# Eight weight pieces of each sub-layer split in buffers of their own, and the products with 1/s spaced out

## The chip, the cores and the metric

The kernel runs on one core of one Trainium2 chip. The metric is the device time of one execution in microseconds. The kernel before takes 1218.72 us, the median of three runs (1218.52 to 1219.39). The profile and its trace come from one further execution of the same kernel.

## The reference

The reference is one inference step of a two-layer encoder trunk for two groups of tokens that share the weights: 256 prompt frames with 16 meta tokens ahead of them, and 32 frames of a running stream. Together that is N = 304 columns of activations with 1024 features, all in 32-bit floats. Cut to what matters:

```python
for l in range(DEPTH):                                     # DEPTH = 2
    x = x + 0.5 * rmsnorm(swiglu(rmsnorm(x, pre1) @ w1_in) @ w1_out, post1)   # D_FF = 2816
    z = rmsnorm(x, pre_mix) @ w_in                         # q, k, v of attention; q, k, v, gate of retention
    x = x + rmsnorm(concat(attention(z), retention(z)) @ w_out, post_mix)
    x = x + 0.5 * rmsnorm(swiglu(rmsnorm(x, pre2) @ w2_in) @ w2_out, post2)
y = rmsnorm(x, final_norm)
```

Attention is windowed, with 8 heads over 2 key/value heads and a learned sink per head. Retention has 8 heads with a decay per head and a state that is given and returned. Key and value caches and states are outputs too.

## The kernel before, in words

Activations lie transposed: features on the 128 partitions, the 304 columns of tokens along the free dimension. Layer 1 drops the 16 meta columns after its mixer's projections and goes on with 288. Each sub-layer (ffn1, mixer, ffn2 of each layer) is a row of groups of matmuls. `group4` makes four blocks of 128 output features over all blocks of input features; `group2` makes two.

Every product is computed in three matmuls, `mm3` (L234, L235, L237): the weight is split into `hi`, its rounded part, and `lo`, the rest, and so is the activation; hi·hi, lo·hi and hi·lo are summed in PSUM. A **piece** is one 128x512 block of weights, 12 matmuls. There are 648 pieces, in the fixed order of the program, two to a **chunk** of 512 KB. `load_to` issues the chunks from SP (L167, L171) into four `raw` buffers: a new chunk's load waits until the split of the chunk four before it is done. `split_one` splits a piece: ACT copies `raw` into `hi` (L183), then DVE subtracts to make `lo` (L186). `hi` and `lo` have ten buffers each, used in turn.

The order of the work is written out by hand: each engine's queue holds its instructions in the order in which the program issues them. `tick(ns)` is called between pieces with a nominal duration. It adds to a clock of the planner, issues up to two splits (`advance`) as long as no more than eight pieces are split and not yet used (`AHEAD`), and issues what is due in `later`, a list of things to do from a given value of that clock. The clock exists only while the program is built; on the chip nothing waits for it. `st["cap"]` keeps the splits back while a norm is under way.

Between sub-layers stands the norm. `Post` is its first half. While the last group of a sub-layer runs its last blocks, `done0` and `done1` take the squares on ACT (L488, L501; tiles `sq`, two buffers) and add them into `acc`, on POOL for the first four blocks (L491) and on DVE for the others (L503). `finish` sums `acc` over the partitions with matmuls by ones (L509, L510) and takes the root, s (L514). The matmuls of the next sub-layer start from x·s: `first` and `step` scale x by s (POOL, L523) and add the sub-layer's output, and `pre_norm` makes the split activations (`act_hi` L401, `act_lo` L404) and the next sum of squares. Because x is carried scaled by s, `unscale` (L545) multiplies it back with 1/s later: one reciprocal on DVE (L547) and eight products on POOL (L549). In the mixer it is due 3000 on the planner's clock after `gate_out`, so in the first of the two `w_out` groups; in an ffn, 3000 after the start of the down projections; in the last ffn, at the third gate/up group.

At the end of an ffn `hold` issues 12 matmuls (L271) that keep TensorE at work. At the end of the mixer the retention states are computed there instead (`states`, L787), and `state_out` sends them on during the next sub-layer, with four transfers between partitions on SP (L804).

In each ffn the hidden activations `hh`, `hl` and the temporaries stand in a pool `ffn`; in the mixer all tiles stand in a pool `mix`, which is closed by `after` when the next norm has been issued. Both pools follow one another in the same room.

Of the kernel before, what the change touches and what calls it, by code (L numbers as in the profile page):

```python
# [15 lines left out]
P = 128  # L16
# [50 lines left out]
UNSCALE = 3000  # L67
# [39 lines left out]
def tile_hybrid_step(ctx, tc, I, O):  # L107
# [35 lines left out]

    for l in range(DEPTH):
        ch_ffn_in(I["ffn1_w_in"][l])
        ch_cols(I["ffn1_w_out"][l], 512, KF)
        ch_cols(I["ffn1_w_out"][l], 0, KF)
        ch_qkv(I["w_in"][l])
        for c0 in (C_Q + 256, C_RK, C_RQ, C_RV, C_RK + 256, C_RQ + 256, C_RV + 256, C_G, C_G + 256):
            ch_pair(I["w_in"][l], c0)  # L150
        ch_cols(I["w_out"][l], 512, KD)
        ch_cols(I["w_out"][l], 0, KD)
        ch_ffn_in(I["ffn2_w_in"][l])
        ch_cols(I["ffn2_w_out"][l], 512, KF)
        ch_cols(I["ffn2_w_out"][l], 0, KF)

    raws, split = {}, {}
    st = {"dma": 0, "split": 0, "use": 0, "free": 0, "cap": 1 << 30, "ramp": 0}
# [318 lines left out]
    class Post:  # L477
# [67 lines left out]
        def unscale(self):  # L545
            rs = small("rs")
            DVE.reciprocal(out=rs[:, T0:], in_=self.s[:, T0:])  # L547
            for k in range(KD):
                POOL.tensor_tensor(out=x[:, k, T0:], in0=x[:, k, T0:], in1=rs[:, T0:], op=ALU.mult)  # L549


    def ffn(pre, post, nxt, prev, after=None):
# [5 lines left out]
        with tc.tile_pool(name="ffn", bufs=1, reuse_waits="tile") as fp:  # L558
# [3 lines left out]
            if last:  # L562
                fin.start(fp)
            state = {}
# [138 lines left out]
    def mixer(l, prev):  # L703
# [5 lines left out]
        mp = mix.enter_context(tc.tile_pool(name="mix", bufs=1, reuse_waits="tile"))  # L709
        def tl(name, shape, dt=F32, tag=None, bufs=1):  # L710
            return mp.tile(shape, dt, tag=tag or name, bufs=bufs, name=name)

# [30 lines left out]
        def rotate(bk, i, dst):  # L743
            t1 = tl("t1", [P, 2, N], bufs=2)
            t2 = tl("t2", [P, 2, N], bufs=1)
            t3 = tl("t3", [P, 2, N], bufs=1)
# [43 lines left out]
        def state_out(b):  # L790
            sa, sb = tl("t1", [P, 2, N], bufs=2), tl("t1", [P, 2, N], bufs=2)
            sc, stt = tl("t2", [P, 2, N]), tl("t3", [P, 2, N])
            sa, sb, sc, stt = (t.rearrange("p a n -> p (a n)")[:, 0:8 * HD].rearrange("p (w q d) -> p w q d", w=2, q=4)
                               for t in (sa, sb, sc, stt))
# [14 lines left out]
        def done_rv(i):  # L809
            def f(m, bk):  # L810
                zr = tl("zr", [P, N], bufs=2)
# [68 lines left out]
        def norm(p):  # L880
# [3 lines left out]
            sd = tl("gsd", [P, N], bufs=2)[:, t0:]  # L884
# [5 lines left out]
        def done_kv(m, bk):  # L890
            if m == 0:
                y = bk[0]
                zk = tl("zk", [P, N])
# [7 lines left out]
                def tr():  # L901
# [6 lines left out]
                    kt = tl("kt", [P, 2, P])  # L908
# [6 lines left out]
            else:  # L915
                zv = tl("zv", [P, N])
# [37 lines left out]
        def softmax(parts, rows):  # L954

            pt = tl("pt", [P, 2, 2, 208], bufs=2)
            sm = tl("sm", [P, 3, 2, 2], bufs=2)
# [22 lines left out]
        def attn_pair(g, c0):  # L980
# [17 lines left out]
            def trans():  # L998
                pT = tl("pT", [P, 2, 2, 2, P], bufs=2)
# [32 lines left out]
        def side_unit(q, n, t0, sink, meta):  # L1032
# [17 lines left out]
            def trans():  # L1050
                b = bank()
                pT = tl("pT", [P, 2, 2, 2, P], bufs=2)[:, 0]
# [43 lines left out]
        def done_g(i):  # L1096
            def f(m, bk):
                if m == 0:
                    zgs.append(tl("zg", [P, 2, N], tag="t1", bufs=2))
# [13 lines left out]
        first = group4(KD, xh, xl, N, (2, 3, 0, 1), lambda m, bk: stats() if m == 0 else None, lead=2)  # L1113
        done_kv(0, first[2:])
# [19 lines left out]
        later.append((clock[0] + UNSCALE, prev.unscale))  # L1134
# [49 lines left out]
```

## Time and profile before

| | |
|---|---|
| median of three runs | 1218.72 us |
| the profiled execution | 1219.73 us |
| its span, first to last instruction | 1218.0 us |
| mean granted TensorE clock | 0.994 |
| TensorE matmuls busy | 1180.7 us (97%) |
| VectorE busy | 826.5 us (68%) |
| ScalarE busy | 593.1 us (49%) |
| GpSimd busy | 194.6 us (16%) |
| moved by DMA | 182.51 MB, mean 150 GB/s |

Times in the trace are microseconds from the start of the span. PE is TensorE's matmul, PEld its weight load, DVE VectorE, ACT ScalarE, POOL GpSimd, SP the engine that issues most loads; "SPq" is its queue. L12 is line 12 of the kernel before. A busy TensorE is not one at its peak, since matmuls are pipelined.

### The profile page before, as it was taken

The page shows a single profiled execution, that of the slowest core. Times are in us where ns is not written, and L with a number is a line of the kernel's source. Part 1 is how long each engine was busy: PE and PEld are TensorE (multiplying, and loading weights), DVE is VectorE, ACT ScalarE, POOL GpSimd, SP SyncE. Part 2 cuts the span into 40 slices and gives each one's busy share as a digit, 9 for nine tenths or more (in the row PEclk, how much of TensorE's full clock was granted, in tenths as well). Part 3 has the DMA queues.
Part 4 walks back from the last instruction along what each step waited for, and adds up shares of the span by engine and source line. Part 5 has one row for each costly group of instructions (what it writes and reads, how often), then busy time and mean ns, then how long its engine had stood idle before and what let it go on. Part 6 is the DMA issues. An engine that isn't in the chain of part 4 may idle for free. (4 is left out here: it accounts for less than half of the span.)

```text
span 1218.0 us, 22795 instructions
## 1 busy us (share of the span) xinstructions
PE 1180.7 (97%) x8716; PEld 1147.9 (94%) x8716; DVE 826.5 (68%) x1491; ACT 593.1 (49%) x1211; POOL 194.6 (16%) x205
## 2 busy tenths in 40 slices
PE   8999999999998999999999999999999989999995
PEld 8999999998898999999989999998989988999995
DVE  6866654497777866675387665746877788766543
ACT  6644444365445545444354544444654554554442
POOL 4200001130216200012030000313101463000000
PEclk9999999999999999999999999999999999999998
DMA  7655465554423554545526455554534336645531
GB/s 227 177 172 167 139 191 156 166 142 118 124 80 119 171 177 139 169 162 158 171 70 208 139 159 177 167 157 140 177 97 125 105 99 195 208 140 177 186 105 39
DMA packets 155309, 182.51 MB, mean 150 GB/s; under 512 B 12016, under 2 KB 125984, under 8 KB 154944
## 3 DMA queue, kind: packets, MB, share of 16 engines
q1 hardware_dynamic: 153488, 178.84, 48.1%
q0 software_dynamic: 1344, 1.76, 0.7%
q8 instruction: 68, 1.11, 0.4%
q10 hardware_dynamic: 368, 0.47, 0.1%
q14 instruction: 41, 0.34, 0.1%
HBM read 175.70 MB, written 2.23 MB: 146 GB/s over the span
## 5 line engine op out<-in xcount | busy, mean ns | idle before, releaser
L234 PE MATMUL bk<-act,hi 128*128 128x304 f32 (+1 forms) x1824 | 555.1, 306 | 5.7 <-ACT act L401 2.9
L235 PE MATMUL bk<-act,lo 128*128 128x304 f32 (+1 forms) x1824 | 543.9, 300 | 2.8 <-DVE lo L186 2.8
L186 DVE TENSOR_TENSOR lo<-raw,hi 128x512 fp32r<-128x512 f32 x648 | 443.8, 730 | 136.0 <-ACT hi L183 132.7
L237 PE MATMUL bk<-act,hi 128*128 128x304 f32 (+1 forms) x1824 | 523.5, 301 | 5.5 <-DVE act L404 4.8
L183 ACT ACTIVATE hi<-raw 128x512 fp32r<-128x512 f32 x647 | 370.0, 622 | 154.5 <-PE bk L237 122.4
L234 PEld LDWEIGHTS bk<-act,hi 128*128 128x128 f32 x1824 | 342.9, 188 | 15.5 <-ACT act L401 5.0
L235 PEld LDWEIGHTS bk<-act,lo 128*128 128x128 f32 x1824 | 343.0, 188 | 5.5 <-DVE lo L186 4.6
L237 PEld LDWEIGHTS bk<-act,hi 128*128 128x128 f32 x1824 | 335.1, 188 | 10.1 <-DVE act L404 9.6
L234 PE MATMUL bk<-hh,hi 128*128 128x304 f32 (+1 forms) x704 | 210.7, 300 | 0.0
L235 PE MATMUL bk<-hh,lo 128*128 128x304 f32 (+1 forms) x704 | 210.2, 299 | 0.0
L237 PE MATMUL bk<-hl,hi 128*128 128x304 f32 (+1 forms) x704 | 207.8, 301 | 0.0
L570 ACT ACTIVATE sg<-tg 128x304 f32<-128x304 f32 (+1 forms) x88 | 40.0, 455 | 191.8 <-DVE tg L569 191.8
L234 PEld LDWEIGHTS bk<-hh,hi 128*128 128x128 f32 x704 | 132.5, 188 | 0.0
L235 PEld LDWEIGHTS bk<-hh,lo 128*128 128x128 f32 x704 | 132.3, 188 | 0.0
L237 PEld LDWEIGHTS bk<-hl,hi 128*128 128x128 f32 x704 | 131.0, 188 | 0.0
L569 DVE TENSOR_TENSOR tg<-bk,rb 128x304 f32<-128x304 f32 (+1 forms) x88 | 41.0, 466 | 82.9 <-PE bk L237 82.8
L549 POOL TENSOR_TENSOR x<-x,rs 128x304 f32<-128x304 f32 (+1 forms) x40 | 44.7, 1152 | 318.5 <-DVE rs L547 171.6
L574 DVE TENSOR_TENSOR hl<-tu,hh 128x304 fp32r<-128x304 f32 (+1 forms) x88 | 41.5, 472 | 46.0 <-ACT hh L573 46.0
L573 ACT ACTIVATE hh<-tu 128x304 fp32r<-128x304 f32 (+1 forms) x88 | 40.0, 455 | 61.6 <-DVE tu L572 61.6
L491 POOL TENSOR_TENSOR acc<-acc,sq 128x304 f32<-128x304 f32 (+1 forms) x18 | 15.0, 833 | 320.4 <-ACT sq L488 319.5
L572 DVE TENSOR_TENSOR tu<-tu,sg 128x304 f32<-128x304 f32 (+1 forms) x88 | 43.7, 496 | 14.3 <-ACT sg L570 9.7
L523 POOL TENSOR_TENSOR x<-x,s 128x304 f32<-128x304 f32 (+1 forms) x35 | 31.3, 929 | 125.0 <-ACT s L521 125.0
(231 smaller groups left out, 848.9 us busy)
## 6 DMA issues: line engine op xcount, KB each, us to landing
raw<-in_ffn_w_in_dram SPq DMA_DIRECT2D x352, 256.0 KB, 4.6
raw<-in_ffn_w_out_dram SPq DMA_DIRECT2D x88, 512.0 KB, 4.6
raw<-in_w_in_dram SPq DMA_DIRECT2D x36, 512.0 KB, 4.0
raw<-in_w_out_dram SPq DMA_DIRECT2D x16, 512.0 KB, 3.9
raw<-in_w_in_dram SPq DMA_DIRECT2D x16, 256.0 KB, 3.1
dec<-in_dec_dram SPq DMA_DIRECT2D x2, 1280.0 KB, 7.0
t<-t SPq DMA_DIRECT2D x24, 76.0 KB, 2.1
out_dram<-xgm SPq DMA_DIRECT2D x2, 384.0 KB, 3.6
```

The lines of the kernel that those rows point to most:

```text
L183: ACT.activation(out=hi, in_=r, func=ACTF.Copy)
L186: DVE.tensor_tensor(out=lo, in0=r, in1=hi.bitcast(F32), op=ALU.subtract)
L234: PE.matmul(out=out, lhsT=a, rhs=xh, start=first, stop=False)
L235: PE.matmul(out=out, lhsT=b, rhs=xh, start=False, stop=False)
L237: PE.matmul(out=out, lhsT=a, rhs=xl, start=False, stop=last)
L523: POOL.tensor_tensor(out=x[:, j, T0:], in0=x[:, j, T0:], in1=self.s[:, T0:], op=ALU.mult)
L549: POOL.tensor_tensor(out=x[:, k, T0:], in0=x[:, k, T0:], in1=rs[:, T0:], op=ALU.mult)
L569: DVE.tensor_tensor(out=tg[:, T0:], in0=bk[j][:, :n], in1=rb[:, T0:], op=ALU.mult)
L570: ACT.activation(out=sg[:, T0:], in_=tg[:, T0:], func=ACTF.Silu)
L572: DVE.tensor_tensor(out=tu[:, T0:], in0=tu[:, T0:], in1=sg[:, T0:], op=ALU.mult)
L573: ACT.activation(out=hh[a][:, T0:], in_=tu[:, T0:], func=ACTF.Copy)
L574: DVE.tensor_tensor(out=hl[a][:, T0:], in0=tu[:, T0:], in1=hh[a][:, T0:].bitcast(F32), op=ALU.subtract)
```

## The change

The first eight pieces of every sub-layer but the first (`edges`, `extra`) are split into 16 tiles of a pool of their own, `xw`, instead of the ten buffers in turn. They do not count among the eight pieces that may be ahead, so that up to 16 pieces can be split when a sub-layer starts. A piece of this kind is split only while `xw` is open. `open_extra` stands behind the gate/up groups in an ffn (not in the last) and behind `gate_out` in the mixer. `close_extra` stands behind the first group of the sub-layer that uses the pieces.

To have the room, the mixer's temporaries move from `mix` to a pool `mtmp`, opened after `close_extra` and closed before `open_extra`; `state_out` uses the room of `qr` and `kr` instead of three temporaries; and the last ffn's tiles for the final norm (`fin.start`, with the load of `gf`) are opened at the second gate/up group.

`unscale` still makes 1/s at once, but puts the eight products into `later`, each 1500 on the planner's clock behind the one before. It is called right behind `gate_out` in the mixer, and 1500 instead of 3000 after the start of the down projections in an ffn.

```diff
-UNSCALE = 3000
+UNSCALE = 1500
+EXTRA = 8
...
+    edges = []
     for l in range(DEPTH):
+        if l:
+            edges.append(2 * len(chunks))
         ch_ffn_in(I["ffn1_w_in"][l])
...
+        edges.append(2 * len(chunks))
         ch_qkv(I["w_in"][l])
...
+        edges.append(2 * len(chunks))
         ch_ffn_in(I["ffn2_w_in"][l])
...
+    extra = {b + j for b in edges for j in range(EXTRA)}
+    ring = [0]
+    for i in range(2 * len(chunks)):
+        ring.append(ring[-1] + (i not in extra))
+    xw = []
+
+    def open_extra():
+        xw.append(ExitStack())
+        st["xw"] = xw[-1].enter_context(tc.tile_pool(name="xw", bufs=1, side="right", reuse_waits="tile"))
+
+    def close_extra():
+        st["xw"] = None
+        xw.pop().close()
...
-        hi = wp.tile([P, 512], F32R, tag="hi", bufs=BUFS, name="hi")
-        lo = wp.tile([P, 512], F32R, tag="lo", bufs=BUFS, name="lo")
+        if i in extra:
+            hi, lo = (st["xw"].tile([P, 512], F32R, name=f"{nm}{(i - 132) % 8}") for nm in ("xhi", "xlo"))
+        else:
+            hi, lo = (wp.tile([P, 512], F32R, tag=nm, bufs=BUFS, name=nm) for nm in ("hi", "lo"))
...
     def advance(most=2):
-        while most and st["split"] < min(st["free"] + AHEAD, 2 * len(chunks)) and st["split"] < st["cap"]:
+        while most and st["split"] < min(st["cap"], 2 * len(chunks)) and ring[st["split"] + 1] - ring[st["free"]] <= AHEAD and (
+                st["split"] not in extra or st["xw"]):
             split_one()
             most -= 1
...
         def unscale(self):
             rs = small("rs")
             DVE.reciprocal(out=rs[:, T0:], in_=self.s[:, T0:])
+
+            def part(k):
+                POOL.tensor_tensor(out=x[:, k, T0:], in0=x[:, k, T0:], in1=rs[:, T0:], op=ALU.mult)
             for k in range(KD):
-                POOL.tensor_tensor(out=x[:, k, T0:], in0=x[:, k, T0:], in1=rs[:, T0:], op=ALU.mult)
+                later.append((clock[0] + UNSCALE * k, lambda k=k: part(k)))
+            later.sort(key=lambda e: e[0])
...
             for g in range(KF // 2):
                 if g == 1:
+                    if prev:
+                        close_extra()
+                    if last:
+                        fin.start(late.enter_context(tc.tile_pool(name="late", bufs=1, reuse_waits="tile")))
...
             if prev and not last:
                 later.append((clock[0] + UNSCALE, prev.unscale))
+            if not last:
+                open_extra()
             p = Post(post, nxt)
...
+        def tt(name, shape, dt=F32, tag=None, bufs=1):
+            if not short:
+                short.append(mtmp.enter_context(tc.tile_pool(name="mtmp", bufs=1, reuse_waits="tile")))
+            return short[0].tile(shape, dt, tag=tag or name, bufs=bufs, name=name)
...
         first = group4(KD, xh, xl, N, (2, 3, 0, 1), lambda m, bk: stats() if m == 0 else None, lead=2)
+        close_extra()
...
         gate_out()
-        later.append((clock[0] + UNSCALE, prev.unscale))
+        mtmp.close()
+        open_extra()
+        prev.unscale()
         p = Post((3, l), (4, l))
```

## Rows read from the trace of the kernel before

**Rows 1.** The page, part 1: busy us (share of the span), instructions

```profile
PE 1180.7 (97%) x8716; PEld 1147.9 (94%) x8716; DVE 826.5 (68%) x1491; ACT 593.1 (49%) x1211; POOL 194.6 (16%) x205
```

**Rows 2.** Waits of TensorE, whole span: us in total, times, longest

```profile
PE bk L509 <- DVE acc L503: 4.9, 5, 2.2
PE bk L237 <- DVE act L404: 4.8, 11, 1.0
PE bk L234 <- ACT act L401: 2.9, 8, 0.6
PE bk L235 <- DVE lo L186: 2.8, 5, 0.9
PE bk L234 <- ACT hi L183: 2.3, 3, 1.1
```

**Rows 3.** Timeline of TensorE: start, us, what, [idle before <- releaser]

```profile
373.14 0.41 PE L235 MATMUL bk<-act,lo 128*128 128x304 f32 x1 [0.86 <-DVE lo L186]
379.48 0.78 PE L509 MATMUL bk<-acc,ones 128*128 128x304 f32 x2 [2.08 <-DVE acc L503]
380.70 3.83 PE L787 MATMUL bk<-vt,k 128*64 128x64 f32 x56
410.76 0.41 PE L234 MATMUL bk<-act,hi 128*128 128x304 f32 x1 [0.55 <-ACT hi L183]
1007.22 0.40 PE L234 MATMUL bk<-act,hi 128*128 128x288 f32 x1 [1.09 <-ACT hi L183]
1007.95 0.40 PE L235 MATMUL bk<-act,lo 128*128 128x288 f32 x1 [0.33 <-DVE lo L186]
1033.82 0.40 PE L234 MATMUL bk<-act,hi 128*128 128x288 f32 x1 [0.70 <-ACT hi L183]
```

**Rows 4.** Timeline of ACT, end of the mixer of layer 0

```profile
370.73 0.42 ACT L488 ACTIVATE sq<-bk 128x304 f32<-128x304 f32 x1 [8.78 <-POOL acc L491]
371.05 1.15 ACT L183 ACTIVATE hi<-raw 128x512 fp32r<-128x512 f32 x2
372.21 1.28 ACT L1138 ACT_TABLE_LOAD   x1
373.51 3.24 ACT L183 ACTIVATE hi<-raw 128x512 fp32r<-128x512 f32 x6
376.65 0.71 ACT L501 ACTIVATE sq<-bk 128x304 f32<-128x304 f32 x2
```

**Rows 5.** Timeline of DVE, same stretch

```profile
358.45 1.29 DVE L186 TENSOR_TENSOR lo<-raw,hi 128x512 fp32r<-128x512 f32 x2
359.66 2.05 DVE L547 RECIPROCAL rs<-s 128x304 f32<-128x304 f32 x1
361.62 4.37 DVE L186 TENSOR_TENSOR lo<-raw,hi 128x512 fp32r<-128x512 f32 x4
...
374.17 3.70 DVE L186 TENSOR_TENSOR lo<-raw,hi 128x512 fp32r<-128x512 f32 x6 [0.49 <-ACT hi L183]
```

**Rows 6.** Timeline of POOL, same stretch

```profile
361.78 8.11 POOL L549 TENSOR_TENSOR x<-x,rs 128x304 f32<-128x304 f32 x8 [10.86 <-DVE rs L547]
369.85 2.68 POOL L491 TENSOR_TENSOR acc<-acc,sq 128x304 f32<-128x304 f32 x3
```

**Rows 7.** Timeline of ACT, end of ffn1 of layer 0

```profile
228.09 0.63 ACT L183 ACTIVATE hi<-raw 128x512 fp32r<-128x512 f32 x1 [1.03 <-PE bk L237]
232.34 0.42 ACT L501 ACTIVATE sq<-bk 128x304 f32<-128x304 f32 x1 [3.62 <-PE bk L237]
```

**Rows 8.** The raw loads that SP issues from 373 to 380: duration ns, landing

```profile
L167 SPq DMA_DIRECT2D raw<-in_ffn_w_in_dram x8: 539/580/605, 373.7 to 378.7; - x8
...
DMA to landing us min/median/max: 3.1/4.5/5.5
```

**Rows 9.** Two stretches: us, busy by engine, PEclk, DMA share, GB/s

```profile
375.00:380.00 5.00, 2.92 (x23) 2.54 (x23) 4.30 (x9) 3.85 (x10) 0.00 (x0) 1.00 0.89 256
...
1006.00:1011.00 5.00, 3.58 (x25) 3.24 (x25) 3.16 (x6) 3.11 (x6) 0.00 (x0) 1.00 1.01 341
```

**Rows 10.** Stretches behind L509, of layer 0 and of layer 1; columns as above

```profile
381.00:382.00 1.00, 1.00 (x21) 1.00 (x20) 0.77 (x3) 0.39 (x2) 0.00 (x0) 0.51 1.01 333
382.00:383.00 1.00, 1.00 (x21) 1.00 (x20) 0.44 (x1) 0.33 (x1) 0.59 (x1) 0.50 0.73 214
...
978.00:980.00 2.00, 2.00 (x55) 2.00 (x55) 1.41 (x3) 0.87 (x2) 0.45 (x1) 1.00 0.91 300
```

**Rows 11.** Timeline of TensorE, end of the mixer of layer 1

```profile
976.71 0.75 PE L509 MATMUL bk<-acc,ones 128*128 128x288 f32 x2 [2.22 <-DVE acc L503]
...
977.88 2.40 PE L787 MATMUL bk<-vt,k 128*64 128x64 f32 x56
```

More of the change, by code (lines that the diff above doesn't have):

```diff
@@ L155, in tile_hybrid_step @@
         ch_cols(I["ffn2_w_out"][l], 0, KF)
+    extra = {b + j for b in edges for j in range(EXTRA)}
[9 more added lines that the diff above has]
+        xw.pop().close()
     raws, split = {}, {}
-    st = {"dma": 0, "split": 0, "use": 0, "free": 0, "cap": 1 << 30, "ramp": 0}
+    st = {"dma": 0, "split": 0, "use": 0, "free": 0, "xw": None, "cap": 1 << 30, "ramp": 0}
     def load_to(c, between=lambda: None):
@@ L557, in ffn @@
         n = N - T0
-        with tc.tile_pool(name="ffn", bufs=1, reuse_waits="tile") as fp:
+        with tc.tile_pool(name="ffn", bufs=1, reuse_waits="tile") as fp, ExitStack() as late:
             tmp = {nm: [fp.tile([P, N], F32, name=f"{nm}{i}") for i in range(2)] for nm in ("tg", "sg", "tu")}
@@ L561, in ffn @@
             hl = [fp.tile([P, N], F32R, name=f"hl{j}") for j in range(KF)]
-            if last:
-                fin.start(fp)
-            state = {}
             def pair(g, j, bk):
@@ L743, in rotate @@
         def rotate(bk, i, dst):
-            t1 = tl("t1", [P, 2, N], bufs=2)
-            t2 = tl("t2", [P, 2, N], bufs=1)
-            t3 = tl("t3", [P, 2, N], bufs=1)
+            t1 = tt("t1", [P, 2, N], bufs=2)
+            t2 = tt("t2", [P, 2, N], bufs=1)
+            t3 = tt("t3", [P, 2, N], bufs=1)
             c = 0 if dst is kr else t0
@@ L790, in state_out @@
         def state_out(b):
[L791 to L794, printed above, removed]
+            two = [tl(nm, [P, 4, N]).rearrange("p a n -> p (a n)")[:, 0:16 * HD].rearrange(
+                "p (i w q d) -> p i w q d", i=2, w=2, q=4) for nm in ("qr", "kr")]
+            sa, sb, sc, stt = (t[:, i] for t in two for i in range(2))
             ACT.activation(out=stt, in_=b.rearrange("p (w q d) -> p w q d", w=2, q=4), func=ACTF.Copy)
@@ L810, in f @@
             def f(m, bk):
-                zr = tl("zr", [P, N], bufs=2)
+                zr = tt("zr", [P, N], bufs=2)
                 p = 2 * i + m
@@ L883, in norm @@
             PE.matmul(out=b[:, t0:N], lhsT=blk, rhs=sq, start=True, stop=True)
-            sd = tl("gsd", [P, N], bufs=2)[:, t0:]
+            sd = tt("gsd", [P, N], bufs=2)[:, t0:]
             ACT.activation(out=sd, in_=b[:, t0:N], func=ACTF.Sqrt, scale=1.0 / HD, bias=epst)
@@ L892, in done_kv @@
                 y = bk[0]
-                zk = tl("zk", [P, N])
+                zk = tt("zk", [P, N])
                 DVE.tensor_tensor(out=zk, in0=y[:, :N], in1=rb, op=ALU.mult)
@@ L907, in tr @@
                                      identity=ident)
-                    kt = tl("kt", [P, 2, P])
+                    kt = tt("kt", [P, 2, P])
                     ACT.activation(out=kt[:, 0], in_=b[:, 0:P], func=ACTF.Copy)
@@ L915, in done_kv @@
             else:
-                zv = tl("zv", [P, N])
+                zv = tt("zv", [P, N])
                 DVE.tensor_tensor(out=zv, in0=bk[1][:, :N], in1=rb, op=ALU.mult)
@@ L954, in softmax @@
         def softmax(parts, rows):
-            pt = tl("pt", [P, 2, 2, 208], bufs=2)
-            sm = tl("sm", [P, 3, 2, 2], bufs=2)
+            pt = tt("pt", [P, 2, 2, 208], bufs=2)
+            sm = tt("sm", [P, 3, 2, 2], bufs=2)
             r, np_ = slice(0, rows), len(parts)
@@ L998, in trans @@
             def trans():
-                pT = tl("pT", [P, 2, 2, 2, P], bufs=2)
+                pT = tt("pT", [P, 2, 2, 2, P], bufs=2)
                 bs = [bank() for _ in range(2)]
@@ L1051, in trans @@
                 b = bank()
-                pT = tl("pT", [P, 2, 2, 2, P], bufs=2)[:, 0]
+                pT = tt("pT", [P, 2, 2, 2, P], bufs=2)[:, 0]
                 pcs = ((0, NMETA),) if meta else ((0, P), (P, DEC))
@@ L1098, in f @@
                 if m == 0:
-                    zgs.append(tl("zg", [P, 2, N], tag="t1", bufs=2))
+                    zgs.append(tt("zg", [P, 2, N], tag="t1", bufs=2))
                 DVE.tensor_tensor(out=zgs[i][:, m, T0:], in0=bk[m][:, :N - T0], in1=rb[:, T0:], op=ALU.mult)
```

2 lines of the change are left out of this document (added).

## The prediction

> **What bounds the kernel now.** I read the page first: TensorE is busy for 1180.7 of 1218.0 us [rows 1], so at most 37 us can be won, and part of that lies in the start and the end of the kernel, which the change leaves alone. Next the list of what the matmuls wait for [rows 2]. The reader is to see that no wait in it is long, and that only three kinds have to do with the splitting of weights into hi (ACT, L183) and lo (DVE, L186): L234 on hi, 2.3 us in 3 waits; L235 on lo, 2.8 us in 5; and L509, the sum of squares that ends a sub-layer, on DVE's acc, 4.9 us in 5. The waits for act (L401, L404) belong to the norm between two sub-layers; no split stands in front of those.
>
> Then the timeline of TensorE, for where these waits stand [rows 3]. The first late piece of each mixer is the seventh of the second w_out group (373.14; layer 1 has its twin). Right behind it L509 stands for 2.08 us (layer 1: 2.22 us [rows 11]). The other late pieces are the last of the second gate/up group of ffn2: one at 410.76 in layer 0, and at 1007.22 and 1033.82 in layer 1. The three ffn ends and the mixers' starts show no late piece.
>
> The queues of the w_out stage say why [rows 4 to 6]. At 361.78 POOL begins the eight products with 1/s and holds on for 8.11 us; only at 369.85 come the adds into acc. The square of the fourth column block needs one of two sq buffers, so ACT stands for 8.78 us, until 370.73. ACT takes its queue in order, so the hi of the last w_out pieces stand behind it: that is the wait at 373.14. Then come a table load (1.28 us), six hi in 3.24 us, and only behind them the squares that end the mixer (376.65); DVE does six lo in 3.70 us before its acc adds. So L509 is late because of splits that stand ahead of the closing squares. DVE's lo takes 0.6 us alone (six in 3.70) and 1.1 us beside POOL's products (four in 4.37) [rows 5].
>
> **The change, part by part.** The sum is made against the profiled execution, 1219.73 us (span 1218.0 and 1.7 around it), which is 1.0 us above the median of 1218.72; I carry the difference over to the median.
>
> *Spread of the products.* `later` spaces them in the order of the program, not in time. A product waits only for rs, and POOL has nothing else queued, so POOL still runs them back to back. Two things do change in the mixer. The reciprocal moves ahead of two lo, so rs is ready 1.2 us earlier (these two took 1.29 us of DVE ahead of 359.66 [rows 5]); those two lo come 2 us later, at about 361.1 and 362.3, and are wanted by TensorE at 362.1 and 363.8: no cost, a margin of 1 us. And counting ticks (seven are due by 9300 of the planner's clock, the eighth at 10500 comes behind the first add), the add that frees ACT stands behind seven products instead of eight. Together the square of 370.73 runs at about 368.6, 2.1 us earlier. With that the piece of 373.14 is in time, and 0.9 us of idle go in each layer. In the ffns I cost the move at nothing: there the products run at the start of the down projections, with 44 pieces of matmuls (some 73 us at the 1.67 us of a piece in [rows 7]) before anything reads x, or in the last ffn behind 16 pieces that are split ahead; without that cover it would cost what the add of 369.85 pays, a few us.
>
> *Extra buffers at the ffn ends.* The eight extra pieces have no ring buffer to wait for, so ACT does them as soon as they reach the head of its queue, some 10 pieces before the boundary. Before, hi goes at TensorE's pace there, 0.63 us of work after 1.03 us of waiting [rows 7], and ACT stands for 3.62 us before the first closing square. Eight more hi are 5 us in about 16 us that are 60% empty. Counted tick by tick, 13 pieces of the next sub-layer stand ahead of the first square instead of six. The raws of the last of these are asked for when the sixth extra lo is done, about 9 us before that square is due; even with the 5.5 us of the slowest load in [rows 8] they land over 3 us before it. So no cost; and no gain, since no piece is late behind these boundaries. If that cover were gone, each ffn end would pay what the mixer ends pay next.
>
> *Extra buffers at the mixer ends.* Here the cover is missing. Between the last two column blocks of the first w_out group and the first closing square the program now issues two hi, the table load, and twelve hi instead of six: each of six ticks may take two pieces, and the extra ones take no ring room. Two more follow between the first and second squares. From 368.6: square, two hi and the table load end at 371.3 (by the durations of [rows 4]), twelve hi at 0.54 us end at 377.9 at the earliest, and the first square, 376.65 before, comes 1.2 us late. That is the lower end.
>
> But the raw tiles do not last that long. Four chunks (eight pieces) are loaded ahead, and a chunk's load is issued when the lo of the chunk four before it is done. The fourth chunk waits for the lo of the last w_out piece (about 371.5 now), and the fifth to seventh for lo of the burst itself, at 373.7, 374.9 and 376.1. In the same place before the change, eight loads in a row took 3.1 us for the first and 5.5 us for the last to land, each costing SP 0.58 us to issue [rows 8]; 256 GB/s passed in that stretch [rows 9]. With 4 to 5.3 us the fifth chunk lands at 377.7, the sixth at 379.7, the seventh at 381.9. ACT stands at each with the squares behind it: twelfth hi done at 380.3, first square 380.8, the two hi of the seventh chunk 382.6, their lo 383.3, then the adds and the last square: L509 at 384.1, against 379.48. That is +4.6 us; by the same steps 4.2 us in layer 1 (976.71 before). If loads land at the 341 GB/s of another stretch [rows 9] it is about +2.7. I take 4.3 us per mixer, 8.6 us, near the case whose loads stand in the same place; ends 2.4 and 13 us (half as much again).
>
> *TensorE's clock.* In layer 0 L509's idle time was followed by a fall to the low level (1.2 of 2.4 GHz, granted 0.51 and 0.50 [rows 10]), in layer 1 not (1.00 [rows 10]); the 56 small state products between L509 and the next sub-layer took 3.83 us there against 2.40 us [rows 3, 11], 1.4 us more. With over 7 us idle I put the fall in both layers: +1.4 us; ends 0 and 5 us (L509's own products slow as well).
>
> The Trainium skill, "TensorE: Matmul & The Clock Gate", Part 1, has it that the throttled clock is the default and activity releases it; that speaks against a change that lengthens an idle stretch. The trace agrees in layer 0 and not in layer 1; by the page alone the fall would be certain in both, as I have taken it, and by the trace alone it would be one in two, 0.7 us.
>
> *Behind the mixer ends.* Sixteen pieces are split when ffn2 starts, so between its start and the products of its second group ACT and DVE have no split to do. The three late pieces there go: hi 0.55, 1.09 and 0.70 us, and 0.3 us each for their lo, together 3.3 us of idle. A late start also refills the pipe: after 1007.22 the next product starts 0.73 us on [rows 3], where about 0.4 us is counted busy; some 0.2 us at each of five, 4.4 us in all. I take -4.4; ends -3.3 and -6.
>
> *Moved tiles and the late start of the final tiles.* The temporaries of the mixer take the room when its first group has been read, 5 us before DVE gets to them; gf's load stands behind the state's transfers on SP, while raws for eight more pieces are already in. Nothing, or 1 us.
>
> Sum: +8.6 +1.4 -4.4 = +5.6 (the 0.9 us of each mixer's late piece lie inside L509's time). 1219.7 + 5.6 = 1225.3 by the profiled run, 1224.3 against the median.
>
> **Rivals.** *All splitting waits go.* If the squares are not held up (their data there by 377.3, when the matmuls end), 1.8 us (L235), 4.3 us (L509), 1.4 us (clock in layer 0) and 4.4 us go: 12 us, 1206.8. For it: every one of these waits is late hi, lo or acc, and the squares' blocker is 2.1 us shorter. Against: twelve hi at 0.54 us do not fit between 371.3 and 377. It ends on the other side; it decides by whether the first closing square on ACT comes before or after 377. *The loads keep pace.* ACT alone sets the end: +2.4, a fall of the clock in one layer 0.7, -4.4: -1.3, 1217.4. For it: up to 341 GB/s elsewhere; against: 256 GB/s and 5.5 us in this very place. *The clock stays low.* Longer idle and a low clock through the norm of both mixers' ends: +13 +5 -4.4 = +13.6, 1232. Against: layer 0's clock was back within 4 us.
>
> **Chances.** Forecast 0.50, all waits go 0.27, loads keep pace 0.17, clock stays low 0.06. The forecast's own range is 1220 to 1229; with the others 1207 to 1229 leaves out about 2 in 10. About 0.2% (2.4 us) is what a measurement of this kernel can tell from no change. Faster: 0.27 and a third of loads keep pace, 0.32. Same: the rest of that and the low edge of the forecast, 0.16. Slower: 0.52.
>
> **What would show it.** In the changed kernel: on ACT twelve hi ahead of the mixers' first closing square, several of them with idle time put down to the raw loads; L509 standing for 6 us or more on acc in both layers, and a low clock behind it; no late hi or lo in ffn2; POOL's products still in one run; the ffn ends as before. The prediction fails if that square comes on time (then 1207), or if the late pieces of ffn2 are still there.

## The result, and the profile after

The changed kernel takes 1227.96 us (median of 4 runs, 1227.46 to 1228.38), the kernel before 1218.98 (4 runs, 1218.52 to 1219.39): a ratio of 1.0074, interval 1.0056 to 1.0091. It is slower by 9.0 us. The profiled executions, 1228.38 and 1219.73 us, differ by 8.65 us, their spans by 8.6.

The page after, part 1 (columns as in [rows 1]): no engine has more or less to do, the span is longer.

```profile
PE 1179.8 (96%) x8716; PEld 1148.3 (94%) x8716; DVE 825.1 (67%) x1491; ACT 593.7 (48%) x1211; POOL 193.0 (16%) x205
```

The waits of TensorE after, over the whole span (columns as in [rows 2]; L533, L527, L258, L259, L206 and L209 are the old L509, L503, L234, L235, L183 and L186):

```profile
PE bk L533 <- DVE acc L527: 19.0, 5, 9.5
...
PE bk L259 <- DVE lo L209: 0.8, 2, 0.5
```

The row "on hi" (2.3 us) is gone and "on lo" is down from 2.8 to 0.8: the buffers did what they are for. The 0.8 left are the late pieces of the two w_out stages, from TensorE's timeline:

```profile
372.55 0.41 PE L259 MATMUL bk<-act,lo 128*128 128x304 f32 x1 [0.24 <-DVE lo L209]
...
975.08 0.40 PE L259 MATMUL bk<-act,lo 128*128 128x288 f32 x1 [0.53 <-DVE lo L209]
```

They are less late than before (0.86 us [rows 3] and 0.95), but still late. And the closing sum now waits 19.0 us instead of 4.9. ACT's timeline at the end of layer 0's mixer (columns as in [rows 4]; L512 and L525 are the old L488 and L501) shows what stands ahead of it:

```profile
369.11 0.42 ACT L512 ACTIVATE sq<-bk 128x304 f32<-128x304 f32 x1 [7.54 <-POOL acc L515]
369.43 1.14 ACT L206 ACTIVATE hi<-raw 128x512 fp32r<-128x512 f32 x2
370.59 1.28 ACT L1179 ACT_TABLE_LOAD   x1
371.89 3.24 ACT L206 ACTIVATE xhi<-raw 128x512 fp32r<-128x512 f32 x6
375.64 1.32 ACT L206 ACTIVATE xhi<-raw 128x512 fp32r<-128x512 f32 x2 [0.52 <-DMA raw<-in_ffn_w_in_dram]
378.47 0.63 ACT L206 ACTIVATE hi<-raw 128x512 fp32r<-128x512 f32 x1 [1.51 <-DMA raw<-in_ffn_w_in_dram]
379.26 1.37 ACT L206 ACTIVATE hi<-raw 128x512 fp32r<-128x512 f32 x2 [0.16 <-DMA raw<-in_ffn_w_in_dram]
380.90 0.63 ACT L206 ACTIVATE hi<-raw 128x512 fp32r<-128x512 f32 x1 [0.27 <-DMA raw<-in_ffn_w_in_dram]
381.43 0.41 ACT L525 ACTIVATE sq<-bk 128x304 f32<-128x304 f32 x1
381.74 1.27 ACT L206 ACTIVATE hi<-raw 128x512 fp32r<-128x512 f32 x2
382.91 0.72 ACT L525 ACTIVATE sq<-bk 128x304 f32<-128x304 f32 x2
384.32 0.42 ACT L525 ACTIVATE sq<-bk 128x304 f32<-128x304 f32 x1 [0.69 <-DVE acc L527]
```

Between the table load and the first closing square stand twelve hi (6 + 2 + 1 + 2 + 1) where there were six, and four of the rows say that ACT stood idle for a raw load, 2.5 us in all. The square comes at 381.43 instead of 376.65. Of the loads behind those waits (SP's raw loads from 372 to 380, as in [rows 8]) half took more than 4.7 us:

```profile
L188 SPq DMA_DIRECT2D raw<-in_ffn_w_in_dram x10: 539/578/606, 372.5 to 378.6; - x10
...
DMA to landing us min/median/max: 3.1/4.7/5.2
```

In layer 1 (974 to 983) the same ten loads took longer, and there ACT stood 3.2 us for them instead of 2.5:

```profile
DMA to landing us min/median/max: 3.1/5.6/5.9
```

POOL in the same stretch (as [rows 6]; L574 and L515 are the old L549 and L491), and then DVE (as [rows 5]; L571 is the old L547):

```profile
360.06 8.22 POOL L574 TENSOR_TENSOR x<-x,rs 128x304 f32<-128x304 f32 x7 [9.52 <-DVE rs L571]
368.24 0.84 POOL L515 TENSOR_TENSOR acc<-acc,sq 128x304 f32<-128x304 f32 x1
369.04 0.84 POOL L574 TENSOR_TENSOR x<-x,rs 128x304 f32<-128x304 f32 x1
```

```profile
357.93 2.04 DVE L571 RECIPROCAL rs<-s 128x304 f32<-128x304 f32 x1
359.90 6.87 DVE L209 TENSOR_TENSOR lo<-raw,hi 128x512 fp32r<-128x512 f32 x6
...
372.55 5.14 DVE L209 TENSOR_TENSOR xlo<-raw,xhi 128x512 fp32r<-128x512 f32 x8
```

The products are not spread in time: seven run in one go, and only the eighth stands behind an add. While they run a lo takes 1.15 us (6.87 / 6), behind them 0.64 (5.14 / 8).

TensorE around both closing sums (as [rows 3, 11]; L826 is the old L787), and then the clock of layer 0 (as [rows 10]):

```profile
384.86 1.38 PE L533 MATMUL bk<-acc,ones 128*128 128x304 f32 x2 [8.64 <-DVE acc L527]
386.03 1.22 PE L534 MATMUL bk<-sq,ones 128*128 128x304 f32 x2
387.18 3.73 PE L826 MATMUL bk<-vt,k 128*64 128x64 f32 x56
...
988.12 1.33 PE L533 MATMUL bk<-acc,ones 128*128 128x288 f32 x2 [9.53 <-DVE acc L527]
989.25 1.17 PE L534 MATMUL bk<-sq,ones 128*128 128x288 f32 x2
990.34 2.74 PE L826 MATMUL bk<-vt,k 128*64 128x64 f32 x56
```

```profile
380.00:384.00 4.00, 0.00 (x0) 0.00 (x0) 3.74 (x7) 3.35 (x7) 0.00 (x0) 0.52 1.05 345
384.00:386.00 2.00, 1.14 (x2) 0.84 (x3) 1.41 (x4) 1.46 (x3) 0.00 (x0) 0.50 0.97 263
...
391.00:392.00 1.00, 1.00 (x8) 1.00 (x9) 1.00 (x2) 0.00 (x0) 1.00 (x2) 1.00 0.01 2
```

The low clock was granted during the idle stretch and lay on L533 and L534 themselves: 1.38 and 1.22 us against 0.75 and 0.68 at the full one (a row of the run with filled idle time, below).

The 8.6 us follow from the same marks in both traces: the closing sums L509 and L533 on TensorE, and behind each the first instruction that uses its root, on DVE (L520 before, L544 after).

| mark | before | after | difference | gained or lost since the mark above |
|---|---|---|---|---|
| closing sum, mixer 0 | 379.48 | 384.86 | +5.38 | +5.38 |
| its root used | 381.39 | 387.88 | +6.49 | +1.11 |
| root used, ffn2 of layer 0 | 610.62 | 615.71 | +5.09 | -1.40 |
| closing sum, mixer 1 | 976.71 | 988.12 | +11.41 | +6.32 |
| its root used | 978.56 | 991.03 | +12.47 | +1.06 |
| span | 1218.0 | 1226.6 | +8.6 | -3.87 |

So by these marks 11.7 us are lost ahead of the two closing sums and 2.2 right behind them, and 5.3 come back behind that. The two w_out stages alone lose a little more. DVE's last `act` of gate_out stands right in front of each; before, and then after:

```profile
357.93 0.47 DVE L1111 TENSOR_TENSOR act<-osb,act 128x304 fp32r<-128x304 f32 x1 [0.53 <-ACT act L1110]
...
955.63 0.46 DVE L1111 TENSOR_TENSOR act<-osb,act 128x288 fp32r<-128x288 f32 x1 [0.51 <-ACT act L1110]
```

```profile
357.54 0.47 DVE L1149 TENSOR_TENSOR act<-osb,act 128x304 fp32r<-128x304 f32 x1 [0.53 <-ACT act L1148]
...
960.58 0.46 DVE L1149 TENSOR_TENSOR act<-osb,act 128x288 fp32r<-128x288 f32 x1 [0.51 <-ACT act L1148]
```

From there to the closing sum layer 0 loses 5.8 us (5.38 + 0.39) and layer 1 6.5 (11.41 - 4.95), 12.2 together. The rest are small differences ahead of the stages: the profiled execution of the changed kernel is 0.45 us late already at the end of the first ffn (235.38 against 234.93), where the runs with the same buffers there stand between 234.28 and 235.15; then 0.8 and 0.2 us are gained in the mixers ahead of w_out.

### The profile page after: what moved, and what is told of

Its sections match the earlier page's. It is cut to its first block, busy times and chain, and to the rows that moved or that the text cites. A ratio compares the mean times of both kernels' runs of the same rounds, so it can differ in the third digit from the quotient of the medians.

```text
span 1226.6 us, 22759 instructions
## 1 busy us (share of the span) xinstructions
PE 1179.8 (96%) x8716; PEld 1148.3 (94%) x8716; DVE 825.1 (67%) x1491; ACT 593.7 (48%) x1211; POOL 193.0 (16%) x205
## 3 DMA queue, kind: packets, MB, share of 16 engines
q8 instruction: 68, 1.11, 0.4%
## 5 line engine op out<-in xcount | busy, mean ns | idle before, releaser
L209 DVE TENSOR_TENSOR lo<-raw,hi 128x512 fp32r<-128x512 f32 x608 | 419.1, 733 | 131.8 <-ACT hi L206 128.0
L258 PE MATMUL bk<-act,hi 128*128 128x304 f32 (+1 forms) x1664 | 504.8, 305 | 0.3 <-ACT act L425 0.3
L259 PE MATMUL bk<-act,lo 128*128 128x304 f32 (+1 forms) x1664 | 496.0, 300 | 0.8 <-DVE lo L209 0.8
L261 PE MATMUL bk<-act,hi 128*128 128x304 f32 (+1 forms) x1664 | 479.1, 300 | 1.3 <-DVE act L428 1.3
L206 ACT ACTIVATE hi<-raw 128x512 fp32r<-128x512 f32 x607 | 348.1, 622 | 143.4 <-PE bk L261 104.7
L258 PEld LDWEIGHTS bk<-act,hi 128*128 128x128 f32 x1664 | 312.9, 188 | 5.9 <-issue 3.5
L259 PEld LDWEIGHTS bk<-act,lo 128*128 128x128 f32 x1664 | 313.0, 188 | 2.0 <-DVE lo L209 1.5
L261 PEld LDWEIGHTS bk<-act,hi 128*128 128x128 f32 x1664 | 306.7, 188 | 2.0 <-DVE act L428 2.0
L258 PE MATMUL bk<-hh,hi 128*128 128x304 f32 (+1 forms) x704 | 210.7, 300 | 0.0
L259 PE MATMUL bk<-hh,lo 128*128 128x304 f32 (+1 forms) x704 | 210.2, 299 | 0.0
L258 PEld LDWEIGHTS bk<-hh,hi 128*128 128x128 f32 x704 | 132.5, 188 | 0.0
L259 PEld LDWEIGHTS bk<-hh,lo 128*128 128x128 f32 x704 | 132.3, 188 | 0.0
L574 POOL TENSOR_TENSOR x<-x,rs 128x304 f32<-128x304 f32 (+1 forms) x40 | 46.6, 1197 | 309.6 <-DVE rs L571 309.6
L515 POOL TENSOR_TENSOR acc<-acc,sq 128x304 f32<-128x304 f32 (+1 forms) x18 | 15.7, 870 | 322.6 <-ACT sq L512 321.8
L547 POOL TENSOR_TENSOR x<-x,s 128x304 f32<-128x304 f32 (+1 forms) x35 | 31.3, 930 | 140.9 <-PE bk L295 109.3
L258 PE MATMUL bk<-act,xhi 128*128 128x304 f32 (+1 forms) x160 | 49.6, 315 | 2.8 <-ACT act L425 2.6
```

Source lines behind the costliest of these rows:

```text
L258: PE.matmul(out=out, lhsT=a, rhs=xh, start=first, stop=False)
L259: PE.matmul(out=out, lhsT=b, rhs=xh, start=False, stop=False)
L261: PE.matmul(out=out, lhsT=a, rhs=xl, start=False, stop=last)
L515: POOL.tensor_tensor(out=self.acc[:, T0:], in0=self.acc[:, T0:], in1=sq[:, T0:], op=ALU.add)
L547: POOL.tensor_tensor(out=x[:, j, T0:], in0=x[:, j, T0:], in1=self.s[:, T0:], op=ALU.mult)
```

## The experiments

The theory is the prediction's: at a mixer's end the extra pieces cost nothing by themselves, but their hi stand ahead of the closing squares in ACT's queue, and the last of them wait there for loads. The rivals: the low clock, the products on POOL, or something in the moved tiles. The kernel before ran at 1218.98 to 1219.78 beside these runs. All edits are of the changed kernel unless the text says otherwise.

### Extra buffers at the ffn ends alone

```diff
-    extra = {b + j for b in edges for j in range(EXTRA)}
+    extra = {b + j for b in edges for j in range(EXTRA) if b not in (192, 516)}
```

> The changed kernel without extra pieces at the two mixer ends (kept at the three ffn ends; the rest of the change kept). Theory (the extra hi queue ahead of the mixers' closing squares and wait there for raw loads): the waits of TensorE for the closing sum fall from some 9 us to under 1 us in each mixer, the low clock behind them goes, the late pieces of ffn2 come back (about 5 us), and the time is 1214 to 1216 us, below the kernel before by the earlier square of the w_out stage. Rival (the moved reciprocal and products, or the moved tiles, are what delays the mixer ends): the waits stay, and the time is 1227 to 1230 us.

1215.46 us (1214.99 to 1215.94), ratio 0.9969 (0.9957 to 0.9981). All of the loss is in the extra pieces of the two mixer ends: without them the change is 3.7 us faster than the kernel before beside it (1219.17). Its waits:

```profile
PE bk L533 <- DVE acc L527: 4.6, 5, 1.9
...
PE bk L258 <- ACT hi L206: 1.7, 2, 1.1
PE bk L259 <- DVE lo L209: 1.4, 4, 0.5
```

One late piece of ffn2 is back in each layer, the one at the end of the second gate/up group. The third, at 1033.82 before, is not. So not all of the 5.3 us belongs to the extra pieces of the mixer ends. In layer 0 ffn2 takes 229.23 us from root to root, as before, against 227.83 in the changed kernel: 1.4 us. In layer 1, from the root to the end of the span, it is 239.44 before, 237.59 here and 235.57 in the changed kernel: 2.0 us belong to these pieces and 1.9 came without them. The spread products alone (below) have 0.9 of the 1.9 (238.54); what brings the rest was not separated.

L533 still waits up to 1.9 us, where I had expected under 1: its squares came earlier, and so did the matmuls ahead of it. I had also expected the low clock to go. In layer 0 it did; in layer 1, behind 1.90 us of idle time, the granted clock still fell to 0.50.

### The same buffers, six pieces ahead of the squares

This keeps every buffer and holds only the issue of the hi: a cap during the last w_out columns, lifted behind the squares.

```diff
+        st["cap"] = st["use"] + 14
...
+        st["cap"] = 1 << 30
+        advance(2)
```

> The changed kernel, all buffers and moves kept, but with the splits of the second w_out group held at six (as before the change) until its closing squares are issued. Theory (what costs is the place of the extra hi in ACT's queue, ahead of the squares): TensorE waits for the closing sum some 2 us as without extra pieces at the mixer ends, and since the pieces are then as late as before, the late pieces of ffn2 come back: 1214 to 1217 us. Rival (opening the extra room or the longer row of splits costs by itself): over 1220 us.

1216.0 us (1215.08 to 1216.62), 0.9968 (0.9955 to 0.9981). On ACT's timeline the first row has six xhi, the squares follow at once, and two xhi come behind the last of them:

```profile
371.25 3.23 ACT L206 ACTIVATE xhi<-raw 128x512 fp32r<-128x512 f32 x6
374.39 0.71 ACT L525 ACTIVATE sq<-bk 128x304 f32<-128x304 f32 x2
...
377.15 1.14 ACT L206 ACTIVATE xhi<-raw 128x512 fp32r<-128x512 f32 x2
```

With the buffers and the moved tiles kept, and only the issue of the splits changed, 12 us are back. So the moved tiles are not the cause; the splits ahead of the squares in ACT's queue are. As expected this order gives up the gain as well: L533 waits as in the run before (4.6 us), and the late pieces of ffn2 are back (hi 1.7 us, lo 1.4).

### Half as many, or more raw tiles

```diff
-EXTRA = 8
+EXTRA = 4
```

> The changed kernel with four extra pieces instead of eight. Ten hi instead of twelve then stand ahead of the first closing square and none between the first two. Theory (raw loads hold these hi): the last load needed is the fifth chunk instead of the seventh, so the closing sum comes about 4 us earlier in each mixer: 1219 to 1223 us. Rival (it is the work on ACT alone, 0.54 us a hi): four hi less before the last square give back some 2 us in each mixer, 1223 to 1225 us.

1222.44 us (1221.82 to 1222.95), 1.0026 (1.0016 to 1.0035). L533 stands 12.7 us in 5 waits, at most 6.2, and in layer 0 it starts at 381.93, 2.9 us earlier than with eight (2.5 from ffn1's closing sum on, and 3.3 in layer 1). That lies between theory (4) and rival (2), and ACT's timeline says why: four hi less are 2.2 us of work, and its waits for loads ahead of the last square fall only from 2.5 to 1.9 us in layer 0 and from 3.2 to 2.1 in layer 1. So most of what four extra pieces cost there is the work itself, and the smaller part the loads. No hi or lo is late in ffn2: four extra pieces are enough there.

```diff
-RAWS = 4
+RAWS = 5
```

> The changed kernel with five raw tiles instead of four, so each chunk is asked for two pieces earlier. Theory (raw loads hold the hi): the closing sum comes one step of the loads, about 1.5 us, earlier in each mixer: 1224 to 1226 us. Rival (the work on ACT alone): no change, 1228 us.

1224.86 us (1224.64 to 1225.09), 1.0045 (1.0029 to 1.0062). One more raw tile takes 1.4 us off L533 in layer 0 (383.46; 1.0 from ffn1's closing sum on, and 2.1 in layer 1). The loads are part of the cost; how large a part this run doesn't settle, since 1.9 us of load waits are left on ACT ahead of the last square (2.5 after).

### TensorE kept busy in the idle stretch

Sixty products that nobody reads run ahead of the closing sum, so that the clock does not fall.

```diff
+        for _ in range(5):
+            hold(*st["last"])
         p.finish()
```

> The changed kernel with 60 products of no use put on TensorE between the end of w_out and the closing sum, some 8 us that fill its idle time. Theory (1.1 us of each mixer end is the low clock on the closing sum's own products): these products run at full clock, the root comes 1.1 us earlier, 1225 to 1226 us, while the closing sum itself starts when it did. Rival (the clock costs nothing, the state products hide it): 1228 us or, if the fill is too long, more.

1228.7 us (1226.65 to 1230.24), 1.0076 (1.0059 to 1.0093): no better. TensorE's timeline:

```profile
375.95 8.55 PE L295 MATMUL bk<-act,hi 128*128 128x304 f32 x60
384.81 0.75 PE L533 MATMUL bk<-acc,ones 128*128 128x304 f32 x2 [0.31 <-DVE acc L527]
385.39 0.68 PE L534 MATMUL bk<-sq,ones 128*128 128x304 f32 x2
386.00 2.40 PE L826 MATMUL bk<-vt,k 128*64 128x64 f32 x56
```

L533 starts when it did (384.81 against 384.86), so the clock is no cause of the wait. Its root is used 1.2 us earlier in each mixer (386.70 against 387.88, 989.84 against 991.03): that is the clock's price at the place. But L533 of layer 1 starts at 988.02, as late as after (988.12), so the first 1.2 us had been lost again by then, and the medians show no gain. The loss lies in layer 1's mixer: from ffn1's closing sum to its own it takes 147.65 us, after 146.66. Of these 1.0 us, 0.6 are there already at ACT's fourth square of w_out (130.92 against 130.30 from the same mark), ahead of that layer's idle stretch. What took them I did not find; for the whole time this run is inconclusive.

### The products alone

On the kernel before, without extra buffers: the products moved behind gate_out and spread, as the change has them; and moved alone, all eight at once.

```diff
-        later.append((clock[0] + UNSCALE, prev.unscale))
+        prev.unscale()
```

> The kernel before with the edit of the products with 1/s alone (reciprocal right behind gate_out, products 1500 of the planner's clock apart); no extra pieces. Theory (this edit gains by the earlier square, and the extra pieces at the ffn ends do nothing): the same time as with extra pieces at the ffn ends only, 1215 to 1216.5 us. Rival (the extra pieces at the ffn ends are worth something): 1217 to 1219 us.

> The kernel before with the reciprocal and all eight products issued right behind gate_out in the mixers, not spaced (the ffns as before). Theory (spacing acts by the order of the queue alone: one product, 0.8 to 1.0 us, goes from behind the first add to ahead of it): 0.5 to 1 us per mixer more than with the spacing, 1216.5 to 1218 us, with POOL's products in one run in both. Rival (the spacing itself relieves DVE): no better than the kernel before, 1219 us or more.

Spread: 1217.63 us (10 runs, 1216.73 to 1218.84), 0.998 (0.9971 to 0.999); L509 waits 4.3 us in 5. At once: 1218.71 (10 runs, 1217.74 to 1220.78), 0.9995 (0.9985 to 1.0004); L509 waits 4.9. So the spread, with the ffns' part of the edit, is worth 1.1 us, and the earlier place by itself nothing that can be told; I had expected more of both, and both came out in the range of the rival or next to it. For the earlier place the trace gives a reason: POOL's eight products take 9.03 us beside six lo, where they took 8.11 beside four [rows 5, 6], so that the first add starts only 0.8 us earlier (369.02 against 369.85).

The 2.2 us between the medians of the spread alone and of the run with ffn ends alone (1215.46; 1.3 us by the ratios) belong to the rest of the change (ffn-end buffers, moved tiles). In the traces 0.7 of it lies in layer 0's mixer, where TensorE's waits for ACT's `pT` in attention fall from 0.9 us to 0.2, and 1.0 behind layer 1's mixer (238.54 against 237.59); layer 1's mixer itself is 0.7 slower, with the low clock behind its closing sum. Which part of the change does it I did not separate.

### A third sq buffer

If POOL's hold on ACT is what starts the pile-up, a third buffer should end it: the fourth square then needs no add.

```diff
-ap.tile([P, N], F32, tag="sq", bufs=2, name="sq")
+ap.tile([P, N], F32, tag="sq", bufs=3, name="sq")
```

> The changed kernel with three sq buffers instead of two, so that the fourth square of the first w_out group need not wait for POOL. Theory (the extra hi start late because ACT stands at that square, and then run into the raw loads): ACT goes on some 6.5 us earlier, the closing sum comes 4 to 5 us earlier in each mixer, 1216 to 1219 us. Rival (the number of hi ahead of the squares decides, whenever they start): under 2 us per mixer, 1224 to 1228 us.

1225.79 us (1225.5 to 1225.88), 1.0047 (1.003 to 1.0064). A miss: I had expected 1216 to 1219. ACT's timeline:

```profile
361.40 0.42 ACT L512 ACTIVATE sq<-bk 128x304 f32<-128x304 f32 x1 [0.34 <-PE bk L261]
...
367.65 1.27 ACT L206 ACTIVATE xhi<-raw 128x512 fp32r<-128x512 f32 x2 [1.57 <-DMA raw<-in_ffn_w_in_dram]
...
373.63 1.37 ACT L206 ACTIVATE xhi<-raw 128x512 fp32r<-128x512 f32 x2 [2.77 <-DMA raw<-in_ffn_w_in_dram]
...
378.95 1.33 ACT L206 ACTIVATE hi<-raw 128x512 fp32r<-128x512 f32 x2 [1.54 <-DMA raw<-in_ffn_w_in_dram]
380.19 0.41 ACT L525 ACTIVATE sq<-bk 128x304 f32<-128x304 f32 x1
```

The fourth square runs 7.7 us earlier, and the first closing square only 1.2. Most of what ACT wins it waits again at raw loads: 8.2 us ahead of the first closing square, against 2.5 after. A load is issued when an earlier lo has read its raw tile, and in this stretch DVE's six lo still share their time with POOL's products (6.88 us, as after). So there seem to be two doors by which the products hold up the stage: the adds that free sq, and the lo that free raw. My theory had only the first. The next run tests the second.

### The products out of the stage

The call that queues the products, moved from behind gate_out to ahead of the mixer's gate groups, closes both doors: POOL does them while it would be idle.

```diff
+        prev.unscale()
         group2(xh, xl, n, done_g(0))
...
-        prev.unscale()
```

> The changed kernel with the reciprocal and the products with 1/s issued ahead of the two gate groups of the mixer, some 13 us earlier, so that POOL is free in the w_out stage. Theory (the products hold the adds, the adds hold the square, the square holds the extra hi, and beside the products each lo takes 1.1 us): the fourth square does not wait, the extra pieces are done before the closing squares, TensorE waits for the closing sum under 2 us, no late piece in w_out or ffn2: 1207 to 1211 us. Rival (raw loads alone set the end): the closing sum comes 4 us earlier at most, 1217 us or more.

1214.84 us (1213.78 to 1215.31), 0.9957 (0.9942 to 0.9972). ACT's fourth square comes at 361.88, about as in the run before (361.40), but the first closing square 5.8 us earlier (374.41 against 380.19): that is the second door, the loads behind the lo. DVE's six lo now take 3.70 us and are done at 361.1 instead of 366.3. Of these 5.1 us, 3.2 are the lo themselves, and 2.0 the reciprocal, which no longer stands ahead of them on DVE; the run changes both, so the products' share of the second door is not all of it. Yet the closing squares still stand behind a late load:

```profile
373.14 1.36 ACT L206 ACTIVATE hi<-raw 128x512 fp32r<-128x512 f32 x2 [1.37 <-DMA raw<-in_ffn_w_in_dram]
374.41 0.41 ACT L525 ACTIVATE sq<-bk 128x304 f32<-128x304 f32 x1
```

L533 waits 7.5 us, at most 3.9. That is 13 us better than the change, but short of the 1207 to 1211 expected: twelve hi still stand ahead of the first closing square and fourteen ahead of the last. With four extra pieces it is ten ahead of both; a further run has a fifth raw tile as well.

```diff
-EXTRA = 8
-RAWS = 4
+EXTRA = 4
+RAWS = 5      (4 in the first of the two)
```

> The changed kernel with the products with 1/s ahead of the gate groups, and four extra pieces instead of eight. Theory: with POOL out of the stage and ten hi, of which the last need the fifth chunk, ahead of the squares, TensorE waits for the closing sum under 1.5 us (3 to 4 us with eight): 1209 to 1212 us. Rival (the four other pieces are wanted in ffn2): late pieces there, 1214 us or more.

> The same with five raw tiles instead of four. Theory (raw loads are what is left): the closing squares come on time as at the ffn ends, 1208 to 1211 us. Rival (no load is late any more): the same time as with four raw tiles.

1207.5 us (1207.24 to 1207.65), 0.9897 (0.9882 to 0.9912), and with the fifth raw tile 1205.98 (1205.62 to 1206.23), 0.9885 (0.9868 to 0.9902). Both are right in direction and faster than I had expected (1209 to 1212, 1208 to 1211). The last is the fastest: 22.0 us below the change and, by its ratio, 1.15% below the kernel before. ACT's timeline in it:

```profile
366.44 3.35 ACT L206 ACTIVATE hi<-raw 128x512 fp32r<-128x512 f32 x6
371.75 0.42 ACT L525 ACTIVATE sq<-bk 128x304 f32<-128x304 f32 x1 [1.96 <-PE bk L261]
```

No hi waits for a load, and ACT now stands idle for TensorE ahead of each closing square (1.96 us ahead of the first, 0.35 to 0.41 ahead of the others; in layer 1 1.28 and 0.32 to 0.38). That is the state in which extra buffers cost nothing. L533 no longer waits in the mixers.

The early products without any extra buffer, on the kernel before and all eight at once, tell what each part is worth:

```diff
+        prev.unscale()
         group2(xh, xl, n, done_g(0))
...
-        later.append((clock[0] + UNSCALE, prev.unscale))
```

> The kernel before with nothing but the reciprocal and the products with 1/s ahead of the gate groups of the mixer; no extra pieces. Theory (the extra pieces are worth the late pieces of ffn2, some 4 to 5 us, once the mixer ends are clean): TensorE waits under 1 us for the closing sum, no late piece in w_out, the late pieces of ffn2 stay: 1211 to 1214 us, some 3 us above four extra pieces with the same edit. Rival (extra pieces are worth nothing): the same as with four extra pieces or less.

1211.43 us (1210.67 to 1212.85), 0.9931 (0.9915 to 0.9947). L509 no longer waits at the mixers' ends; the late pieces stay:

```profile
PE bk L234 <- ACT hi L183: 1.6, 2, 1.1
```

So with POOL out of the stage the change with four extra pieces brings 3.9 us (1211.43 to 1207.5) and with eight loses 3.4 (1211.43 to 1214.84): the same buffers, on either side of the point where ACT's queue is full. The 3.9 hold the rest of the change too. Behind the mixer ends the traces show 1.4 us in layer 0 (229.16 to 227.80 from root to root) and 3.0 in layer 1 (238.60 to 235.65 from the root to the end). Of the 3.0, 1.9 are these pieces' own (237.59 to 235.65, from the run with ffn ends alone).

## Why the prediction was right, and where its sizes were off

*The spread acts by queue order alone: right about the order, too large in size.* Seven products in one run, then an add, as counted. The square forecast at 368.6 came at 369.11. Measured from gate_out's last `act`, it moved 1.2 us earlier in both layers (370.73 to 369.11 with a stage that begins 0.39 earlier, 968.04 to 971.76 with one that begins 4.95 later), not 2.1. The reciprocal and POOL's start are 1.3 us earlier, as computed; but seven products beside six lo take 8.22 us, as long as eight beside four had (8.11 [rows 6]), so the product less gained nothing. Nor is the piece of 373.14 in time: 0.24 us are left of 0.86, and 0.53 of 0.95 in layer 1.

*The mixer ends: right in mechanism, too small.* Twelve hi ahead of the first closing square, four waits at raw loads, the square at 381.43 (forecast 380.8), the closing sum at 384.86 (384.1). The w_out stage of layer 0 lost 5.8 us against a computed 4.6, that of layer 1 6.5 against 4.2, together 12.2 against the 8.6 taken. In each layer 0.9 of it is the square that moved too little. In layer 1 slower loads come on top: landing took 5.6 us in the median and 5.9 at most, where I had reckoned with 4 to 5.3 from layer 0's row, and ACT stood 3.2 us for them. That row gives the fastest, the median and the slowest load; I read it as the first and the last.

*The clock: right that it falls in both layers, wrong in its place.* I charged 1.4 us to the 56 state products of layer 1. Those lie beside the norm and cost next to nothing: with slow ones ffn2 of layer 0 takes 227.83 us from root to root, with the fast ones of the run with filled idle time 227.72 (in layer 0 they had been slow before as well). The price is on the closing sum's own four products, 1.1 us in each layer, 2.2 together. By the rule of the Trainium skill, "TensorE: Matmul & The Clock Gate", Part 1, that the throttled clock is the default and activity releases it, the fall was to come in both; behind idle of 8.6 and 9.5 us the trace agrees.

*ffn2: right that the late pieces go, partly for another reason.* No late hi or lo, and 5.3 us come back against 4.4. But only 3.4 of them go with the extra pieces of the mixer ends (1.4 in layer 0, 2.0 in layer 1). I had put the piece of 1033.82 at the end of the second gate/up group; it stands two groups (16 pieces) behind 1007.22, while sixteen early pieces fill the first two groups only, and it is in time without them as well. The other 1.9 us came without these pieces, from parts of the change that I had put at nothing.

*The ffn ends: right.* Thirteen hi go ahead of ffn1's first closing square. Four times ACT stands there for loads, 3.8 us in all, and it still waits 2.42 us for TensorE ahead of the square (I had computed a margin of over 3):

```profile
232.69 0.42 ACT L525 ACTIVATE sq<-bk 128x304 f32<-128x304 f32 x1 [2.42 <-PE bk L261]
```

*The sum.* Forecast +8.6 +1.4 -4.4 = +5.6. Measured: +12.2 in the w_out stages, +2.2 for the clock, -3.4 for ffn2's late pieces, and -2.4 that I had not forecast (the 1.9 above, 1.0 in the mixers ahead of w_out, less the 0.5 of a late start) = +8.6. The mis-sized term is the closing sum's lateness, 3.6 us too small. The clock (0.8) and ffn2 (1.0) were too low and too hopeful as well; that the total is only 3.0 us off, and inside the range, owes something to luck, since the unforecast gains hide 2.4 of it. The rival "loads keep pace" fell by the four load waits, "all waits go" by the square at 381.43. For "the clock stays low" the clock would have had to stay down through the norm; in layer 0 it was at 1.00 by 391.

*What I had wrong without its showing in the time* is the reason for the crowded queue. I named the adds behind POOL's products as the squares' blocker; the third sq buffer and the products ahead of the stage showed the lo beside those products, with the reciprocal in front of them, to be a blocker of its own, through the raw tiles.

## What to carry to other kernels

Room to work ahead is not free for an engine that takes its queue in order: ask what stands behind the extra work, whether its last input can be there by then, and let it run ahead only in a stretch in which the engine waits for someone else. When removing a stall brings nothing, look for a second path by which the same culprit holds the stage, and move the culprit, not the buffer. Price a low clock on the few products that the next step waits for, not on the many that it does not.

## What the runs showed of the hardware

- A product on POOL and a lo on DVE that run side by side take 1.17 us (8.22 / 7) and 1.15 us; the lo takes 0.62 without the products (3.70 / 6), the eighth product 0.84 where no lo runs. The Trainium skill, "SBUF — State Buffer", section "SBUF: two separate sides", has the two engines share a port pair under an exclusive lock when DVE reads two SBUF inputs. The trace agrees that they hold each other up; but 1.17 us for a pair is less than the 1.46 that the two take one after the other, so it is not all of each instruction that excludes the other.
- A short idle stretch need not decide the clock: behind 2.08 us of it the clock fell in layer 0 of the kernel before, behind 2.22 us in layer 1 it did not [rows 10, 11]. With extra buffers at the ffn ends alone it fell behind 1.90 us in layer 1 (0.50) and not behind 1.81 in layer 0 (1.00).
